# A planned kernel: what the plan charges for TensorE's products and for its changes of tiling

## The chip, the cores and the metric

The kernel runs on one core of one Trainium2 chip. The metric is device time in microseconds (us) of one execution; each time shown is one run, and medians are over runs.

## What is computed

A trunk of two layers over 256 context tokens and 512 latent tokens, 1024 channels, all in fp32. Each layer modulates and normalises its input, projects it once, and feeds three mixers side by side:

```python
conv_l, q_l, k_l, v_l, rw_l, gate_l = _split(hl @ lp['w_in'], IN_SPLITS)
y_att_l = _att_post(_diff_attend(q_lat, keys_l, vals_l, lam), lp['att_subln_g'], lambda_init)
y_conv_l = _conv_branch(conv_l, *conv_args)
y_rw_c, y_rw_l = _rwkv_branch(rw_c, rw_l, lp, need_ctx)
out_l = _merge(y_conv_l, y_att_l, y_rw_l, gate_l, lp)
xl = xl + gl1 * ol
xl = xl + gl2 * _sqrelu_mlp(_modulate(xl, norm2_g[l], shl2, scl2), mlp_w1[l], mlp_w2[l])
```

The three mixers are a depthwise convolution of 31 taps, differential attention with 4 heads, and RWKV-7, a recurrence run in both directions. A gated merge, an output projection and a squared-ReLU MLP follow. The second layer drops the context tokens after they have been read. A last normalisation gives the output, latent tokens alone.

## The kernel before

Activations lie with channels on the 128 partitions and tokens along the free axis. A weight matrix is cut into units of 128 output channels. A unit's product over the 512 latent tokens (and, where the context counts, over its 256) runs as three reduced-precision products: each fp32 operand is split into a high and a low part (wh and wl, hh and hl), and hh*wh, hl*wh, hh*wl are summed in PSUM under the name mmps. The weights come in as wr by DMA, ScalarE copies them to wh, VectorE subtracts to get wl. These big products fill the whole 128x128 array.

RWKV's recurrence is computed in chunks of 64 tokens, by small fp32 products that use a part of the array (64 or 32 rows or columns): lps and aps (low-rank inputs), tps (the matrices of a chunk), tvps, wps and jps (solving them), ca, cb and psy (the chain that carries the state X from chunk to chunk). An fp32 product shows as two records in the trace, a reduced one and a transpose as one. There are 16 halves (8 in each layer), with 6 chunks each. A step of the chain goes ca<-x,ar on TensorE, an addition into rhs on VectorE, ca<-rhs,j and cb<-rhs,j on TensorE, copies into gv, ca<-gv,tok on TensorE, and an addition that makes the next x. The outputs psy of a step are computed in the next step's first wait (y_products).

**How the order is made.** The whole order of all engines is fixed when the program is built. Each part of the work is a generator, a stream, with a letter. `weave` keeps a planned clock for each engine. Again and again it asks every stream when its next piece could start, and lets the earliest one issue; within EPS = 0.02 us the one that stands first in a string of letters wins (ORDER_A = "CIEKAWLRGT" in the RWKV stage of layer 0: C is the chain, K and R prepare chunks, W converts weights, G issues the big products, T the convolution's taps on VectorE). A stream names the time its data is due, the engine, and maybe a lead: the chain gives STICK = 0.2 us ahead of the groups behind rhs and gv, so that it is taken up to 0.2 us before its data is due.

```python
t = max(s[1], self.clock[s[2]] + s[5], held) - s[5]
if best is None or t < at - EPS:
    best, at, got, since = s, t, names, held
```

The stream that is taken issues its instructions and calls `spend`, which moves the engine's planned clock by the piece's charge and returns the end plus SEM = 0.19 us, the time at which others may use the result. The charges are formulas: `Timed.cost` for VectorE, ScalarE and GpSimd (elements / 960, 1200 and the like, plus a constant), `load` for DMAs, `product` and `turn` (a transpose) for TensorE. Only the order that comes out matters: real waits are semaphores.

Before, `product` (L227) charges columns / 2400 us + 0.003 for a reduced product and for an fp32 one four passes, scaled by output width for small ones. A full-width product gets 0.06 us more when the one before it was charged less than 0.1 us (`self.short`). The second of two products that run side by side on different rows (`beside`) is charged 0.004. `turn` (L239) charges 0.119.

The stages in time: a head (0 to 107 us), the RWKV stage woven with the input projection of layer 0 (107 to 595), attention, convolution and the remaining projection units (to about 905), merge, output projection and MLP (to about 1600), the norm and the start of layer 1 (to 1705), its RWKV stage (to 2215), its attention (to 2390), its merge and MLP, and the last norm.

Of the kernel before, what the change touches and what calls it, by code (L numbers as in the profile page):

```python
# [19 lines left out]
P = 128  # L20
# [31 lines left out]
SPARE = 1.5  # L52
EPS = 0.02
STICK = 0.2
BLK = 1040
CTX = (0, NCTX)
LAT = (NCTX, NLAT)
# [63 lines left out]
class Trunk:  # L121
# [15 lines left out]
    def setup(self):  # L137
# [29 lines left out]
        nc.vector.tensor_tensor(out=self.cc, in0=self.cc, in1=sg, op=ALU.mult)  # L167
        self.blk_in = [self.dram.tile([96 * BLK], F32, name=f"bin{i}") for i in range(2)]
        self.blk_out = [self.dram.tile([96 * BLK], F32, name=f"bout{i}") for i in range(2)]
        self.blk = 0  # L170
# [56 lines left out]
    def product(self, out, lhsT, rhs, at=None, beside=0, **kw):  # L227
        self.nc.tensor.matmul(out, lhsT, rhs, **kw)  # L228
        m, n = lhsT.free_size(), rhs.free_size()
        c = n if rhs.dtype == F32R else 4 * n * max(m, 32) / P  # L230
        cost = (max(0.027, c / 2400) + 0.003) if not beside else 0.004
        if rhs.dtype != F32R:
            cost = max(cost, 0.1 if m == P else 0.0) + (0.012 if 32 < n <= P else 0.04 if n > P else 0.0)
        if self.short and m == P:
            cost += 0.06
        self.short = cost < 0.1
        return self.spend("PE", cost, at)

    def turn(self, out, src):  # L239
        self.nc.tensor.transpose(out, src, self.ident)  # L240
        return self.spend("PE", 0.119)

    def load(self, out, in_, q=None, rate=360e3):

# [167 lines left out]
    def start(self):  # L412
        self.queues, self.closing, self.n_queued = [], False, 0
        self.plan, self.after, self.after_over, self.n_after = [], deque(), False, 0
        self.n_load = self.n_conv = self.n_used = 0
        self.banks = dict(lat=deque([0.0, 0.0]), ctx=deque([0.0]))
        self.ring = dict(lat=deque([self.mm, self.mm]), ctx=deque([self.mm]))
        self.gone = dict(lat=deque(), ctx=deque())
        self.raws, self.parts = deque([self.wp] * WR), deque([self.wp] * WC)
        self.locks, self.t0, self.now, self.todo, self.short = {}, 0.0, 0.0, [], False  # L420
        self.shared, self.shared_t = 0, 0.0

    def enqueue(self, i, q):
# [643 lines left out]
    def half_t(self, n, pp, hh, prep, c0):  # L1067
# [38 lines left out]
        def blocks(x):  # L1106
            return x.rearrange("(p x) -> p x", x=BLK)[:, 0:1024].rearrange("p (i w) -> p i w", w=64)[:, :, 0:16]

        def rows(x, g):
            return x[g * 48 * BLK:(g + 1) * 48 * BLK].rearrange("(n y) -> n y", y=4 * BLK)[:, 0:4096].rearrange(  # L1110
                "n (s t) -> s n t", t=64)
# [197 lines left out]
    def chain_piece(self, pi, st, y, need_y):  # L1309
# [5 lines left out]
        for q in range(2):  # L1315
# [11 lines left out]
            else:  # L1327
# [10 lines left out]
                t = V.tensor_tensor(out=rhs, in0=ga[:, 0:128], in1=tv[:, q, :], op=ALU.add)  # L1338
                yield t, "PE", None, None, STICK
            gps = [ga[:, 256:384], gb[:, 0:128]]  # L1340
# [8 lines left out]
            yield from self.y_outs()  # L1349
            yield t, "PE", None, None, STICK  # L1350
            if not last:
# [206 lines left out]
    def phase_a(self, l, full, lat, esh, esf, eps):  # L1558
        nc = self.nc
        c0 = self.c0 = lat[0][0]  # L1560
        with ExitStack() as es:
# [19 lines left out]
            if l == 0:  # L1581
                z = self.pa.tile([P, T], F32, tag="stage", name="zero", bufs=1)[0:96, 0:BLK // 2]
                nc.gpsimd.memset(z, 0.0)
                for t in self.blk_out:
                    for h in range(2):
                        nc.gpsimd.dma_start(out=t.rearrange("(p h x) -> p h x", h=2, x=BLK // 2)[:, h], in_=z)
            self.weave(ORDER_A[l], dict(C=self.chain(l, c0), I=self.inverse(), R=self.prepare(l, c0),
# [732 lines left out]
```

## Time and profile before

| | |
|---|---|
| median of 3 runs | 2911.05 us (2907.64 to 2918.86) |
| the profiled execution | 2907.25 us, its span 2905.5 us |
| instructions | 56275 |
| TensorE busy | 2770.2 us, 95% |
| VectorE busy | 1951.0 us, 67% |
| ScalarE busy | 1298.6 us, 45% |
| GpSimd busy | 105.5 us, 4% |

The span runs from the first to the last instruction of the profiled execution. Matmuls overlap: a big product with 512 columns is recorded for some 0.39 us, while the next one starts 0.23 us later, so what a product costs is read from start to start. "Idle before" is time in which no recorded instruction of the engine ran. PEclk is the granted share of TensorE's full clock of 2.4 GHz.

### The profile page before, as it was taken

Reading aid. Unit: us, or ns where it says so; the run is one execution under the profiler, and the core shown is the slowest. Engines: PE = TensorE matmul, PEld = TensorE weight load, DVE = VectorE, ACT = ScalarE, POOL = GpSimd, SP = SyncE. Lnnn points to the kernel's source line nnn. Section 1 sums busy time; section 2 is a strip of 40 time slices with the busy share of each in tenths; the row PEclk is TensorE's granted clock in tenths of the full one; section 3 lists DMA queues with packets and bytes.
Section 4 is the critical chain, followed back from the end, with each engine's and each line's share of the span. In section 5 each row is a group of like instructions: output and inputs, shape, how many; then the busy total and the mean of one; then the engine's idle time right before and its main releaser. Section 6 shows DMA issues by size and latency. Waiting matters only on the chain.

```text
span 2905.5 us, 56275 instructions
## 1 busy us (share of the span) xinstructions
PE 2770.2 (95%) x22423; PEld 2234.9 (77%) x22423; DVE 1951.0 (67%) x4230; ACT 1298.6 (45%) x2522; POOL 105.5 (4%) x181
## 2 busy tenths in 40 slices
PE   8999999998999999999999999999999889899998
PEld 6777777776788887888888777777777667788887
DVE  6778777489995558764333569889985766644445
ACT  4556655555544224231313346555554663433333
POOL 0000000010000000000000000001000100000000
PEclk9999999999999999999999999999999999999999
DMA  5232223354237733553112313233235436322223
GB/s 211 66 77 70 72 81 90 102 158 120 83 111 267 255 124 111 181 187 110 63 65 68 101 60 91 64 87 83 77 108 177 140 103 203 134 96 95 95 96 104
DMA packets 248903, 333.05 MB, mean 115 GB/s; under 512 B 118385, under 2 KB 124161, under 8 KB 248513
## 3 DMA queue, kind: packets, MB, share of 16 engines
q1 hardware_dynamic: 243312, 313.73, 34.2%
q0 software_dynamic: 3712, 14.17, 1.9%
q8 instruction: 176, 2.88, 0.4%
q10 hardware_dynamic: 1616, 1.56, 0.2%
q14 instruction: 87, 0.70, 0.1%
HBM read 267.37 MB, written 48.65 MB: 109 GB/s over the span
## 4 chain that ended last, share of the span: by engine, by line
PE 72%; DVE 13%; ACT 5%; DMA 3%; issue 2%; SPq 1%; POOL 0%; DVEq 0%; ACTq 0%; POOLq 0%
PE mmps L228 59%; PE ca L228 3%; DVE cacc L92 2%; DVE wl L92 2%; ACT wh L92 1%; PE tps L228 1%; PE sps L228 1%; PE psy L228 1%; PE wps L228 1%; PE jps L228 1%; DVE x L92 1%; DVE ast L92 1%; DMA j<-bout 1%; DMA akm<-akl 1%; PE tvps L228 1%
## 5 line engine op out<-in xcount | busy, mean ns | idle before, releaser
L228 PE MATMUL mmps<-hh,wh 128*128 128x512 f32 (+1 forms) x2344 | 850.0, 363 | 23.9 <-ACT wh L92 5.8
L228 PE MATMUL mmps<-hh,wl 128*128 128x512 f32 (+1 forms) x2344 | 844.8, 360 | 9.0 <-DVE wl L92 8.8
L228 PE MATMUL mmps<-hl,wh 128*128 128x512 f32 (+1 forms) x2344 | 844.3, 360 | 4.1 <-DVE hl L92 3.8
L92 DVE TENSOR_TENSOR wl<-wr,wh 128x512 fp32r<-128x512 f32 x596 | 411.5, 691 | 480.6 <-ACT wh L92 469.0
L92 ACT ACTIVATE wh<-wr 128x512 fp32r<-128x512 f32 x596 | 375.2, 630 | 714.9 <-PE mmps L228 664.9
L228 PEld LDWEIGHTS mmps<-hh,wh 128*128 128x128 f32 x2344 | 447.9, 191 | 95.0 <-issue 18.0
L228 PEld LDWEIGHTS mmps<-hh,wl 128*128 128x128 f32 x2344 | 446.9, 191 | 80.9 <-DVE wl L92 16.2
L228 PEld LDWEIGHTS mmps<-hl,wh 128*128 128x128 f32 x2344 | 447.6, 191 | 67.9 <-DVE hl L92 7.2
L228 PE MATMUL mmps<-ffl,wh 128*128 128x512 f32 (+1 forms) x792 | 279.2, 353 | 0.0
L228 PE MATMUL mmps<-ffh,wh 128*128 128x512 f32 (+1 forms) x792 | 278.1, 351 | 0.0
L228 PE MATMUL mmps<-ffh,wl 128*128 128x512 f32 (+1 forms) x792 | 277.0, 350 | 0.0
L92 DVE SCALAR_TENSOR_TENSOR cacc<-upad,dww,cacc 128x783 f32<-128x783 f32 (+1 forms) x240 | 215.2, 897 | 4.5
L228 PEld LDWEIGHTS mmps<-ffh,wh 128*128 128x128 f32 x792 | 149.1, 188 | 22.7
L228 PEld LDWEIGHTS mmps<-ffh,wl 128*128 128x128 f32 x792 | 148.9, 188 | 21.5
L228 PEld LDWEIGHTS mmps<-ffl,wh 128*128 128x128 f32 x792 | 149.4, 189 | 20.7
L92 DVE SCALAR_TENSOR_TENSOR x<-mmps,mod,x 128x512 f32<-128x512 f32 (+1 forms) x126 | 80.0, 636 | 45.5 <-PE mmps L228 45.0
L92 POOL TENSOR_TENSOR bk<-bk,pc 128x384 f32<-128x384 f32 x64 | 58.0, 937 | 1198.9 <-PE tps L228 1140.0
L92 DVE SCALAR_TENSOR_TENSOR sq<-mmps,rl 128x512 f32<-128x512 f32 x96 | 56.9, 596 | 40.4 <-ACT rl L92 40.4
L92 ACT ACTIVATE stage<-mmps 128x512 f32<-128x512 f32 (+1 forms) x116 | 59.0, 510 | 50.8 <-PE mmps L228 45.9
L92 ACT ACT_TABLE_LOAD x62 | 79.5, 1283 | 4.7 <-PE mmps L228 2.6
L92 DVE TENSOR_REDUCE ast<-sps 128x1 f32<-128x768 f32 (+1 forms) x80 | 65.6, 845 | 21.6 <-PE sps L228 21.5
L92 ACT ACTIVATE rl<-mmps 128x512 f32<-128x512 f32 x96 | 49.3, 515 | 67.9 <-PE mmps L228 67.9
(329 smaller groups left out, 4371.1 us busy)
## 6 DMA issues: line engine op xcount, KB each, us to landing
wr<-in_w_dram SPq DMA_DIRECT2D x268, 256.0 KB, 2.5
wr<-in_win_dram SPq DMA_DIRECT2D x236, 256.0 KB, 2.8
modw<-in_modw_dram SPq DMA_DIRECT2D x80, 512.0 KB, 4.5
wr<-in_pw_dram SPq DMA_DIRECT2D x48, 256.0 KB, 2.9
wr<-in_wo_dram SPq DMA_DIRECT2D x44, 256.0 KB, 2.6
g<-stage SPq DMA_DIRECT2D x24, 384.0 KB, 3.2
gate<-g SPq DMA_DIRECT2D x24, 384.0 KB, 4.0
scb<-in_modw_dram SPq DMA_DIRECT2D x16, 512.0 KB, 6.3
```

Of the source, the lines that this page charges most:

```text
L92: f(**kw)
L228: self.nc.tensor.matmul(out, lhsT, rhs, **kw)
```

## The change

The charges of TensorE in the plan are replaced. A product is `part` when it uses fewer than 128 columns or rows of the array. A change from whole to part is charged ENTER = 0.09 us, from part to whole LEAVE = 0.2 us, in place of the 0.06 us. A column is charged 1/2246 us rather than 1/2400, a transpose 0.108 us. The least charge of an fp32 product is 0.22 us if it uses the whole array, 0.1 us if it is full in width and part in rows (0.1 us for both before), and none beside the general least of 0.024 + 0.003 us (0.027 + 0.003 before) if it is narrow. No instruction, tile or buffer is added or taken away; the order that the weaver makes can differ on every engine.

```diff
@@ -52,6 +52,9 @@
 SPARE = 1.5
 EPS = 0.02
 STICK = 0.2
+
+ENTER = 0.09
+LEAVE = 0.2
 BLK = 1040
 CTX = (0, NCTX)
 LAT = (NCTX, NLAT)
@@ -227,18 +230,21 @@
     def product(self, out, lhsT, rhs, at=None, beside=0, **kw):
         self.nc.tensor.matmul(out, lhsT, rhs, **kw)
         m, n = lhsT.free_size(), rhs.free_size()
+        part = m < P or lhsT.shape[0] < P
         c = n if rhs.dtype == F32R else 4 * n * max(m, 32) / P
-        cost = (max(0.027, c / 2400) + 0.003) if not beside else 0.004
+        cost = max(0.024, c / 2246) + 0.003 if not beside else 0.004
         if rhs.dtype != F32R:
-            cost = max(cost, 0.1 if m == P else 0.0) + (0.012 if 32 < n <= P else 0.04 if n > P else 0.0)
-        if self.short and m == P:
-            cost += 0.06
-        self.short = cost < 0.1
+            cost = max(cost, 0.0 if m < P else 0.1 if part else 0.22) + (0.012 if 32 < n <= P else 0.04 if n > P else 0.0)
+        if part != self.part:
+            cost += ENTER if part else LEAVE
+            self.part = part
         return self.spend("PE", cost, at)
 
     def turn(self, out, src):
         self.nc.tensor.transpose(out, src, self.ident)
-        return self.spend("PE", 0.119)
+        cost = 0.108 + (LEAVE if self.part else 0.0)
+        self.part = False
+        return self.spend("PE", cost)
 
     def load(self, out, in_, q=None, rate=360e3):
 
@@ -417,7 +423,7 @@
         self.ring = dict(lat=deque([self.mm, self.mm]), ctx=deque([self.mm]))
         self.gone = dict(lat=deque(), ctx=deque())
         self.raws, self.parts = deque([self.wp] * WR), deque([self.wp] * WC)
-        self.locks, self.t0, self.now, self.todo, self.short = {}, 0.0, 0.0, [], False
+        self.locks, self.t0, self.now, self.todo, self.part = {}, 0.0, 0.0, [], False
         self.shared, self.shared_t = 0, 0.0
 
     def enqueue(self, i, q):
```

## Rows read from the trace of the kernel before

**Rows 1.** The page: the span, and its part 1 (busy time by engine).
```profile
span 2905.5 us, 56275 instructions
...
PE 2770.2 (95%) x22423; PEld 2234.9 (77%) x22423; DVE 1951.0 (67%) x4230; ACT 1298.6 (45%) x2522; POOL 105.5 (4%) x181
```

**Rows 2.** Windows by stage: stretch, length, busy us (x records) by engine, PEclk, DMA.
```profile
107.00:595.00 488.00, 469.21 (x6345) 368.95 (x6343) 349.92 (x1022) 270.77 (x591) 34.83 (x57) 0.99 0.32 85
1705.00:2215.00 510.00, 494.29 (x6091) 370.29 (x6091) 438.11 (x1166) 275.72 (x595) 33.79 (x48) 1.00 0.31 85
2215.00:2390.00 175.00, 150.51 (x641) 112.41 (x641) 122.43 (x199) 109.13 (x199) 18.57 (x36) 0.92 0.52 153
1200.00:1600.00 400.00, 400.00 (x2285) 350.54 (x2284) 180.78 (x292) 102.20 (x169) 0.64 (x2) 1.00 0.31 106
```

**Rows 3.** Timeline of TensorE at 2700 us: start, us, instruction.
```profile
2700.16 0.40 PE L228 MATMUL mmps<-ffl,wh 128*128 128x512 f32 x1
2700.39 0.39 PE L228 MATMUL mmps<-ffh,wl 128*128 128x512 f32 x1
```

**Rows 4.** Timeline of TensorE, 433 to 437 us: one step of the chain.
```profile
433.66 0.44 PE L228 MATMUL ca<-x,ar 128*64 128x128 f32 x4
434.03 0.38 PE L228 MATMUL mmps<-hh,wl 128*128 128x256 f32 x1
434.25 0.28 PE L228 MATMUL mmps<-hh,wh 128*128 128x256 f32 x1
...
434.72 0.28 PE L228 MATMUL mmps<-hl,wh 128*128 128x256 f32 x1
434.93 0.27 PE L228 MATMUL ca<-rhs,j 64*64 64x64 f32 x1
...
435.31 0.38 PE L228 MATMUL mmps<-hh,wl 128*128 128x256 f32 x1
435.53 0.28 PE L228 MATMUL mmps<-hh,wh 128*128 128x256 f32 x1
...
435.86 0.45 PE L228 MATMUL ca<-gv,tok 128*64 128x64 f32 x8
```

**Rows 5.** Timeline of VectorE, 430 to 436.5 us.
```profile
430.85 0.56 DVE L92 TENSOR_TENSOR bk<-t,e 128x384 f32<-128x384 f32 x1
431.33 0.55 DVE L92 TENSOR_TENSOR bk<-a,e 128x384 f32<-128x384 f32 x1
...
434.31 0.28 DVE L92 TENSOR_TENSOR rhs<-ca,tv 128x128 f32<-128x128 f32 x1
```

**Rows 6.** Groups of TensorE's instructions: count | busy, mean ns | idle before, releasers.
```profile
L228 PE MATMUL ca<-gv,tok 128*64 128x64 f32 x704 | 40.5, 235 | 1.7 <-ACT gv L92 1.6
...
L228 PE MATMUL ca<-rhs,j 64*64 64x64 f32 x352 | 38.8, 230 | 5.0 <-DVE rhs L92 4.0
L228 PE MATMUL ca<-x,ar 128*64 128x128 f32 x352 | 38.6, 297 | 1.2 <-DVE x L92 0.9
```

**Rows 7.** Timeline of TensorE: first and last entry into small tiles, 365 in all.
```profile
107.91 1.16 PE L228 MATMUL tps<-ar,bk 64*128 64x128 f32 x16
...
2212.44 0.34 PE L228 MATMUL psy<-tr,gv 128*64 128x64 f32 x4
```

**Rows 8.** Waits of TensorE: what waited, for what: us, times, longest us.
```profile
PE mmps L228 <- DVE wl L92: 9.9, 12, 3.2
...
PE sps L228 <- DMA akl<-akl: 6.6, 5, 2.9
PE sps L228 <- ACT ap L92: 5.9, 7, 1.8
PE mmps L228 <- ACT wh L92: 5.8, 5, 3.3
...
PE atps L240 <- ACT aat L92: 4.2, 6, 1.3
PE atps L240 <- DVE ap L92: 4.2, 3, 2.9
```

## The prediction

> **What bounds the kernel now.** I read the page first: TensorE is busy 2770.2 of 2905.5 us, so it idles 135.3 us and no other engine is near it [rows 1]. The reader is to see there that only three things can move the time: TensorE's idle time, time at the low clock, and time lost at changes of tiling. Its products themselves stay the same, as the change edits charges in the plan and not one instruction.
>
> Next the windows by stage [rows 2]. "Phase A" is the stretch in which RWKV's small products are woven between the big ones of the input projection: 107 to 595 us in layer 0 and 1705 to 2215 us in layer 1. TensorE is busy 469.21 of 488 and 494.29 of 510 us there, so it waits 34.5 us in both, at a granted clock of 0.99 and 1.00 (2.4 GHz nearly all the time). Attention of layer 1 (2215 to 2390 us) waits 24.5 of 175 us, and its granted clock is 0.92. In the MLP (1200 to 1600 us) it never waits.
>
> Then the timeline, for pitches. Two big products with 512 columns start 0.23 us apart [rows 3], with 256 columns 0.12 us (434.25 onward) [rows 4]. Entering the small tiles costs extra: the last big product before them starts at 434.72, the first small one at 434.93, 0.21 us against 0.12, so 0.09. Leaving costs 0.22 against 0.12 behind the first big product (435.31 to 435.53), and about 0.10 more ahead of it: 0.2. These are the numbers that the new constants hold.
>
> **What the plan believed, and will believe.** One step of the chain, from 433.66 to 435.86 [rows 4], took 2.20 us. An fp32 product shows as two records, so the four records of ca<-x are two products. Old charges: 2 x 0.122 for ca<-x, 6 x 0.110 for the six big products, 4 x 0.068 for the rhs group, 0.06 + 3 x 0.110 for the last three: 1.56 us, 71% of the real time. New charges: 2 x 0.129, 0.2 + 6 x 0.117, 0.09 + 4 x 0.072, 0.2 + 3 x 0.117: 2.09 us, 95%. Summed in this way over all products of both phase A stretches [rows 2], the old charges come to 414 and 431 us, the new ones to 471 and 496, against busy times of 469 and 494. VectorE was already charged its pitch: two 128x384 operations start 0.48 us apart [rows 5], charged 0.47. So the old plan ran TensorE some 15% too fast against the other engines; the new one runs them alike.
>
> TensorE: Matmul & The Clock Gate of the Trainium skill, section "Wait — 56ns, not 53.3ns?", gives N / 2.4 GHz + 2.5 ns, which is 0.216 us at 512 columns: the old charge, and it speaks against the new one. This trace does not agree, its pitch is 0.23 [rows 3]. By the page, the 448 big products that stay in the waits of part 1 below would each be charged 0.015 us too much, an estimate of 7 us more of stalls, and the sum would end at 2912 us; by the row nothing is added.
>
> **Part by part.** The weaver takes the stream that can start first; the cost of a change of tiling is charged only after a choice, so it steers nothing directly. What changes is how many big products fit into a wait of the chain.
>
> 1. Fewer big products per wait. For the groups behind rhs and gv the weaver stops filling STICK, 0.2 us, before the data is due. In the example rhs ends at 434.59 [rows 5] and its group starts at 434.93, a slack of 0.34 us. I went through all groups ca<-x, ca<-rhs and ca<-gv [rows 6] (88, 88 and 88 places) in time; 165 have big products ahead of them. Stopping the fill where the right clock would stop it takes out 132 of 580 big products there (24 us of filling), and the idle time ahead of those groups goes from 5.6 to 8.3 us: **+2.7 us**. The 24 us aren't saved: those products run later, in attention or behind it. Bounds: 0, and 0.2 us for each of the 176 groups with STICK, 35 us. I take 2.7, since it rests on these very places.
>
> 2. Changes of tiling. Phase A enters the small tiles 172 + 193 = 365 times, counted from the first to the last [rows 7], at 0.09 + 0.2 us each. A group that comes ready while TensorE is in small tiles is joined to them. With leaving charged, the plan spends 42% of phase A in or around small tiles rather than 38%; of some 192 groups that don't hang on the chain (per half: lps, aps, three tps, three tvps, four solves; 16 halves) 4% more, eight, join: 8 x 0.29 = **-2.3 us**. Bounds: 0 and 192 x 0.29 = -56; near 0, since nothing in the choice looks for it.
>
> 3. Big products that wait for converted weights. TensorE waits 9.9 us for wl and 5.8 for wh [rows 8]. With the engines' plans in step, fewer conversions stand behind a VectorE or ScalarE operation that is still waiting for a product. Bounds 0 and -15.7; I take a quarter, **-3.9 us**, nearer to 0: only phase A, a third of the span, has charges that change by more than 7%.
>
> 4. Attention. Products here are charged 5% more (130 to 136 us for layer 1), so the cover over each wait shrinks. 21 waits (akl 5, ACT ap 7, aat 6, DVE ap 3) come to 20.9 us [rows 8]. If each was covered for about 3 us, 5% are 0.15 us: 21 x 0.15 = 3.2. Bounds 0 and 3.2; half, **+1.5 us**.
>
> 5. MLP, merge, head: every product scaled alike, so their order and the gaps stay. Nothing, hidden by TensorE's own queue; if that cover were gone, VectorE at 180.78 of 400 us [rows 2] has room.
>
> Sum: +2.7 - 2.3 - 3.9 + 1.5 = -2.0 us. The profiled execution took 2907.25 us around its span of 2905.5, 0.13% under the median of 2911.05. 2907.25 - 2.0 = **2905 us**. A measurement of this kernel can tell about 0.5%, 14.5 us, from no change.
>
> **Rivals.**
>
> *Faster: long waits vanish.* The six waits of [rows 8] hold 36.6 us, and attention of layer 1 loses 175 x 0.08 = 14 us to the low clock of 1.2 GHz that follows them [rows 2]. They come of an order that doesn't fit the real times; a plan in step could undo half of both: 18 + 7 = 25 us, 2882 us. For it: the sums of the new charges meet the busy times within 1%. Against it: these waits lie mostly outside phase A, where the charges change by 5 to 7% alone. Perfetto Trace Analysis of the Trainium skill, "Identifying the Most-Contended Engine", wants TensorE's headroom judged by the weight loads' busy share, not the matmuls'. By it there is more room: weight loads are busy 76% and 73% in phase A against 88% in the MLP, 135 us in all by [rows 2].
>
> *Slower: the old error was a cushion.* As TensorE really ran 15% behind its plan, data was mostly there when it came. With the cushion gone, each of the 176 groups behind rhs and gv can stall for up to STICK. At half of that, 0.1 us, 176 x 0.1 = 18 us and 2925 us; it decides from 14.5 / 176 = 0.08 us each. For it: in the example the new charges put 0.29 us of entering and leaving into a wait whose slack is 0.34. Against it: 48 of the 88 rhs groups have no big product ahead of them at all, small ones fill their wait, and the waits today come to 5.0 and 1.7 us [rows 6].
>
> *It does not do what it says.* The order is largely set by what depends on what. Then the orders differ little and the time is that of before, 2907; this lies within the forecast's case.
>
> **How the numbers follow.** Forecast, no change that can be told: 0.42, its own range 2890 to 2920. Faster rival 0.33, as every charge moves toward the trace. Slower rival 0.25. Range: on the fast side two thirds of the waits and the clock (33 us) give 2874; on the slow side 0.14 us a stall gives 2932; about 0.1 is left beyond either end. Faster by over 0.5% 0.33, within 0.42, slower 0.25.
>
> **What would show it.** Right: phase A is shorter by some 10 us in each layer while fills move behind it; rhs groups wait more than 5.0 us, to about 8; entries into small tiles fall from 365 by about eight; total idle within 10 us of 135. Faster rival: wl, akl and ap waits fall by half and attention's clock rises over 0.92. Slower rival: idle ahead of ca<-rhs and ca<-gv above 20 us. The forecast is wrong if total idle or the number of entries moves by more than a tenth.

## The result: slower by 2.65%, and the profile after

Over six runs the changed kernel takes 2986.81 us (2975.58 to 2996.01) against 2910.30 us of before: a ratio of 1.0265, 95% interval 1.0246 to 1.0283. The forecast was 2905 us with a range up to 2932. Its profiled execution took 2990.15 us, 82.9 us more than the one of before.

The page of the changed kernel, its span and part 1:

```profile
span 2988.4 us, 56305 instructions
...
PE 2806.5 (94%) x22423; PEld 2258.3 (76%) x22423; DVE 1953.1 (65%) x4230; ACT 1296.8 (43%) x2522; POOL 105.0 (4%) x181
```

Against [rows 1]: the same 22423 matmul records, and yet TensorE is busy 36.3 us longer, and idle 46.6 us longer. The other engines do the same work in the same busy time. So all of it is time lost between the same products.

For a comparison stage by stage, both RWKV stages are cut at the same marks now: from the first lps to the last psy. Windows of before, layer 0 and layer 1:

```profile
86.20:562.60 476.40, 460.53 (x6320) 361.83 (x6320) 351.19 (x1040) 264.65 (x587) 30.14 (x48) 1.00 0.29 77
1711.00:2213.00 502.00, 486.29 (x6063) 364.02 (x6062) 433.95 (x1158) 273.36 (x590) 33.79 (x48) 1.00 0.31 84
```

The same windows of the changed kernel:

```profile
84.70:551.20 466.50, 434.89 (x6071) 336.14 (x6071) 345.48 (x1030) 253.34 (x566) 31.37 (x48) 0.97 0.27 69
1765.80:2236.20 470.40, 433.81 (x5765) 321.95 (x5765) 398.37 (x1106) 253.07 (x555) 31.82 (x48) 0.98 0.28 73
```

The stages became shorter, by 9.9 and 31.6 us, which looks like a gain. But 249 and 298 records are missing from them: big products, which now run later. The groups by line show it, one third of the filling each, in layer 0 and then layer 1 of before:

```profile
L228 PE MATMUL mmps<-hh,wh 128*128 128x256 f32 (+1 forms) x443 | 157.0, 354 | 3.6 <-DVE r L92 1.6 <-DVE k L92 0.9 <-DVE stage L92 0.8
L228 PE MATMUL mmps<-hh,wh 128*128 128x512 f32 (+1 forms) x437 | 166.3, 381 | 0.1
```

and of the changed kernel:

```profile
L231 PE MATMUL mmps<-hh,wh 128*128 128x256 f32 (+1 forms) x360 | 129.2, 359 | 3.4 <-DVE k L95 1.6 <-DVE stage L95 0.6 <-DVE r L95 0.5
L231 PE MATMUL mmps<-hh,wh 128*128 128x512 f32 (+1 forms) x339 | 129.1, 381 | 0.0
```

At the pitches of [rows 3, 4], 0.231 us for 512 columns (the median of the MLP) and 0.12 for 256, the filling in both stages is worth 495.9 us before (1614 and 1026 products) and 386.5 after (1218 and 876). That gives the measure used from here on: **the length of both stages less their filling**, that is small products, changes of tiling, waits and clock. It is 978.4 - 495.9 = 482.5 us before and 936.9 - 386.5 = 550.4 after: 68 of the 83 us are lost here. Idle time gives 36.6 of them (from 15.87 + 15.71 to 31.61 + 36.59). The granted clock, 0.97 and 0.98 where it was 1.00, gives about 20: 41 us of these stages run at 1.2 GHz, half of the full clock. Entries into small tiles fell from 174 + 193 to 161 + 179, 27 x 0.29 = 8 us gained, an estimate at the price of [rows 4]. The remaining 19 us are left by subtraction: time between the starts of products that is neither idle nor clock, see the last section.

A good part of the waits is ahead of the chain's groups. The same lines as [rows 6], after:

```profile
L231 PE MATMUL ca<-gv,tok 128*64 128x64 f32 x704 | 44.2, 241 | 5.1 <-ACT gv L95 2.9 <-DVE gv L95 1.5
...
L231 PE MATMUL ca<-x,ar 128*64 128x128 f32 x352 | 40.2, 303 | 9.2 <-DVE x L95 8.0
L231 PE MATMUL ca<-rhs,j 64*64 64x64 f32 x352 | 39.3, 232 | 13.7 <-DVE rhs L95 12.3 <-DVE upad L769 0.5
```

28.0 us ahead of these three groups where it was 7.9: 20.1 of the 36.6 us. VectorE is named for most of it. It isn't slower at its work, it comes late to it: the rhs operation starts a median of 0.54 us after the start of its product's last record, 0.40 before (88 places each; the quickest place has 0.31 in both). But coming late is not enough for a loss: in a kernel below that loses nothing (the change x 0.87) the median is 0.56, and the wait is short all the same.

```profile
L231 PE MATMUL ca<-rhs,j 64*64 64x64 f32 x352 | 38.9, 231 | 6.5 <-DVE rhs L95 5.2
```

What that kernel has more of is filling: 2752 big products in both stages, 2094 in the changed kernel. The timeline of VectorE in the changed kernel, at the step of [rows 4], has an example of a late operation:

```profile
435.21 0.27 DVE L95 TENSOR_SCALAR gv<-cb 64x128 f32<-64x128 f32 x1
436.18 0.75 DVE L95 SCALAR_TENSOR_TENSOR v<-mmps,pvl,v 128x511 f32<-128x511 f32 x1 [0.70 <-ACT v L95]
436.85 0.28 DVE L95 TENSOR_TENSOR x<-ca,xp 64x128 f32<-64x128 f32 x1
```

The product of x (ca<-gv,tok) ended at 436.04. The operation for x stands in VectorE's queue behind one on v that waits 0.70 us for ScalarE, so x starts 0.81 us after its product; in the kernel before, at the same step, 0.12 us after. The order is fixed: one late operation can hold up whatever was planned behind it.

The other 15 us lie mostly in the merge of layer 0, 219.3 us where it took 207.2: its modulation products wait 5.5 us for weights, and the clock falls to 0.98. The stretch from layer 0's RWKV stage to its merge loses about 8 us more, net of filling, and layer 1's merge gains about 7. The merge of layer 0 before and after:

```profile
896.50:1103.70 207.20, 201.56 (x1569) 170.99 (x1568) 114.40 (x205) 63.95 (x104) 0.00 (x0) 1.00 0.60 209
936.00:1155.30 219.30, 208.65 (x1565) 172.02 (x1564) 98.97 (x186) 50.32 (x88) 0.00 (x0) 0.98 0.57 197
```

### The profile page after: what moved, and what is told of

Same layout as the page of the kernel before. It is cut to its first block, busy times and chain, and to the rows that moved or that the text cites. A ratio compares the mean times of both kernels' runs of the same rounds, so it can differ in the third digit from the quotient of the medians.

```text
span 2988.4 us, 56305 instructions
## 1 busy us (share of the span) xinstructions
PE 2806.5 (94%) x22423; PEld 2258.3 (76%) x22423; DVE 1953.1 (65%) x4230; ACT 1296.8 (43%) x2522; POOL 105.0 (4%) x181
## 5 line engine op out<-in xcount | busy, mean ns | idle before, releaser
L231 PE MATMUL mmps<-hh,wh 128*128 128x512 f32 (+1 forms) x2344 | 850.9, 363 | 20.4 <-DVE k L95 6.4
L95 DVE TENSOR_REDUCE ast<-sps 128x1 f32<-128x768 f32 (+1 forms) x80 | 65.4, 845 | 20.4 <-PE sps L231 20.2
L95 DVE TENSOR_TENSOR ffl<-sq,ffh 128x768 fp32r<-128x768 f32 (+1 forms) x64 | 52.8, 825 | 38.8 <-ACT ffh L95 38.6
```

The lines of the kernel that those rows point to most:

```text
L95: f(**kw)
```

## The experiments

Theory 1: all charges of TensorE together set how fast its planned clock runs against the other engines' clocks; slower means less filling in each wait, and the cushion goes. Theory 2: charging the changes of tiling in lumps does it. All times are medians, with the ratio to the kernel before from the same chip. "Loss" is the measure above, less the 482.5 us of before; "fill" counts big products in both stages (2640 before).

| kernel | us | ratio, 95% interval | fill | loss, us |
|---|---|---|---|---|
| the change | 2986.8 | 1.0265, 1.0246 to 1.0283 | 2094 | 68 |
| column pitch alone | 2937.0 | 1.0103, 1.0078 to 1.0128 | 2419 | 28 |
| tiling charges alone | 2947.9 | 1.0138, 1.0115 to 1.0161 | 2410 | 43 |
| the change x 0.87 | 2909.8 | 1.0003, 0.9990 to 1.0017 | 2752 | 6 |
| before x 1.15 | 3007.3 | 1.0342, 1.0315 to 1.0368 | 2308 | 65 |
| the change, SEM 0.30 | 2957.9 | 1.0168, 1.0142 to 1.0193 | 2442 | 41 |
| the change, STICK 0 | 2994.2 | 1.0295, 1.0266 to 1.0325 | 2191 | 63 |
| the change x 0.80 | 2957.1 | 1.0169, 1.0144 to 1.0194 | 2909 | -9 |
| before x 0.90 | 2969.8 | 1.0216, 1.0181 to 1.0251 | 3064 | -5 |
| x 0.87 in the RWKV stages alone | 2927.9 | 1.0072, 1.0054 to 1.0091 | 2752 | 9 |
| the chain taken 0.2 us late | 2991.5 | 1.0295, 1.0263 to 1.0328 | 2204 | 59 |
| VectorE x 1.15 | 2936.2 | 1.0096, 1.0078 to 1.0113 | 2684 | 17 |
| VectorE, ScalarE, GpSimd x 1.15 | 2939.3 | 1.0107, 1.0091 to 1.0124 | 2531 | 26 |
| the change x 0.93 | 2931.3 | 1.0067, 1.0052 to 1.0082 | 2448 | 33 |
| x 0.80 in layer 0's RWKV stage, x 0.87 elsewhere | 2914.6 | 1.0016, 1.0004 to 1.0029 | 2767 | -1 |
| VectorE x 1.15 and SEM 0.30 | 2936.8 | 1.0091, 1.0071 to 1.0111 | 2813 | 9 |

**The two halves of the change.** The column pitch alone, on the kernel before:

```diff
-        cost = (max(0.027, c / 2400) + 0.003) if not beside else 0.004
+        cost = (max(0.027, c / 2246) + 0.003) if not beside else 0.004
```

> The column pitch alone (1/2246 us a column in place of 1/2400), changes of tiling charged as before. Charges of big products rise by 6.5%, of the whole of phase A by about 5%. Theory 1 (the speed of TensorE's planned clock against the other engines sets how much filling lies in each wait, and every slowing of it takes cushion away): a third of the loss, 2930 to 2945 us. Theory 2 (charging changes of tiling in lumps does it): 2905 to 2915 us.

and the changes of tiling alone (ENTER and LEAVE as in the change, in `turn` too):

```diff
-        if self.short and m == P:
-            cost += 0.06
-        self.short = cost < 0.1
+        part = m < P or lhsT.shape[0] < P
+        if part != self.part:
+            cost += ENTER if part else LEAVE
+            self.part = part
```

> ENTER and LEAVE alone, all products at the charges of before. Phase A's charges rise by about 9%. Theory 1 (planned speed of TensorE): two thirds of the loss, 2950 to 2970 us. Theory 2 (the lumps): all of it, 2980 to 2990 us.

2937.0 and 2947.9 us, the second 2 us under the range of theory 1. Each does harm by itself, the one that adds more to the charges the more, and together nearly the whole: 1.03% and 1.38% of 2.65%. The pitch has nothing to do with lumps, so theory 2 fails as the only cause.

**The same proportions at the old speed, and the old proportions at the new speed.** In the changed kernel, and with 1.15 in the kernel before (`turn` alike):

```diff
-        return self.spend("PE", cost, at)
+        return self.spend("PE", 0.87 * cost, at)
```

> The changed kernel with every charge of TensorE times 0.87, ENTER and LEAVE among them: the same proportions, the planned speed of before. Theory 1: 2900 to 2920 us, some 1300 filling products in phase A of layer 0. Theory 2: still 2960 us or more. A third theory (the old charges had proportions that happened to suit the chain): 2940 or more as well.

> The kernel before with every charge of TensorE times 1.15: the old proportions, the planned speed of the changed kernel. Theory 1: 2970 to 3000 us, with fewer than 1150 filling products in phase A of layer 0. Theory 2: 2905 to 2920 us.

These two decide it. Scaled by 0.87, the change costs nothing (1.0003); the old charges scaled by 1.15 lose even more than the change does, a little over what was expected, with 1166 fillings in layer 0 where under 1150 were forecast. Of the 97 us that its profiled execution took more than the one of before, 65 lie in the RWKV stages and 31 between layer 0's RWKV stage and its merge, net of filling. The windows of the scaled change, layer 0 and 1:

```profile
84.40:580.90 496.50, 476.15 (x6379) 374.79 (x6379) 357.60 (x1043) 275.83 (x599) 31.51 (x48) 0.99 0.28 76
1709.60:2220.30 510.70, 495.55 (x6115) 374.09 (x6115) 435.71 (x1163) 277.19 (x597) 33.54 (x48) 1.00 0.32 86
```

and of the kernel before with 1.15:

```profile
86.10:556.30 470.20, 438.12 (x6159) 339.32 (x6158) 348.67 (x1034) 259.79 (x576) 30.22 (x48) 0.99 0.27 70
1765.10:2270.40 505.30, 463.06 (x5893) 343.04 (x5892) 424.81 (x1146) 261.17 (x569) 32.92 (x48) 0.97 0.27 72
```

Length less busy time: 20.4 and 15.2 us in the first, near the 15.9 and 15.7 of before; 32.1 and 42.2 in the second, as in the changed kernel. What the proportions are hardly matters here; how fast the whole planned clock of TensorE runs does.

**Which slack is missing.** Longer hand-overs, and no early commitment, both on the changed kernel:

```diff
-SEM = 0.19
+SEM = 0.3
```

> The changed kernel with SEM, the planned delay from one engine's end to the next engine's start, at 0.30 us in place of 0.19; TensorE's charges stay those of the change. If the loss is that planned waits are too short for the real ones, with TensorE's speed only the old remedy: waits are planned 0.22 us longer per hand-over pair, filling comes back and the time falls to 2900 to 2930 us. If exact charges do harm in another way, it stays above 2960 us.

```diff
-STICK = 0.2
+STICK = 0.0
```

> The changed kernel with STICK = 0, so that the groups behind rhs and gv are taken when their data is due by the plan, no longer up to 0.2 us ahead. If the early commitment to these 176 groups is the loss, 2910 to 2930 us. If every wait of phase A is too tight, the x groups and the solves among them, it falls by a third at most: 2955 to 2975 us.

Longer hand-overs bring back over a third, 2957.9 us, between the two outcomes stated. STICK at 0 brings nothing back, 2994.2 us: less than either theory gave it. So the lead that the forecast blamed in its slower rival isn't the fault by itself. A margin ahead of the chain's own groups is no remedy either:

```diff
-STICK = 0.2
+STICK = -0.2
...
-            yield self.x_t, "PE"
+            yield self.x_t, "PE", None, None, STICK
```

> The changed kernel with the chain's three groups (x, rhs, gv) taken 0.2 us after the planned time of their data, in place of 0.2 us ahead (rhs, gv) and at it (x); all charges those of the change. If it is slack ahead of the chain's own groups that is missing: filling comes back by one or two products at each of 264 places, 2910 to 2935 us. If the delay sits in the other groups too (solves, tps, tvps, weights), 2945 us or more.

2991.5 us, so the delay sits in other groups too, by the expectation. The waits for x are hardly shorter than in the changed kernel (8.0 us there), those for rhs are (12.3 there):

```profile
PE ca L231 <- DVE rhs L95: 7.6, 20, 1.6
PE ca L231 <- DVE x L95: 7.3, 20, 0.7
```

The loss of 59 us stays even so: shorter waits ahead of rhs alone don't win the time back. Charging VectorE more does (in the second kernel the factor holds for ScalarE and GpSimd too):

```diff
-            return self.trunk.spend(self.name, self.cost(op, kw), at)
+            return self.trunk.spend(self.name, self.cost(op, kw) * (1.15 if self.name == "DVE" else 1.0), at)
```

> The changed kernel with VectorE's charges times 1.15, all others those of the change. If VectorE runs behind its plan and the chain's groups wait for its queue, the plan makes room for that: 2920 to 2945 us, stalls ahead of ca<-rhs and ca<-x at 10 us or less. If VectorE's charges are right and any wait is just too tight by chance, less than a third comes back: 2960 us or more.

> VectorE's, ScalarE's and GpSimd's charges times 1.15, TensorE's those of the change: nearly the ratio of before, with SEM and the DMA charges left alone. If the ratio of TensorE to the other engines is all that counts: 2905 to 2925 us. If the hand-over and DMA times must be stretched as well: 2930 to 2955 us.

2936.2 us, two thirds of the loss back, and 51 of the 68 us in the RWKV stages. The waits in the kernel with VectorE x 1.15:

```profile
PE ca L231 <- DVE rhs L95: 7.8, 21, 0.8
PE ca L231 <- DVE x L95: 2.2, 9, 0.3
```

Those for x fall from 8.0 to 2.2 us, those for rhs from 12.3 to 7.8, no further than with the margin; the groups wait 9.2 and 2.9 us in all, a little over the 10 that was expected. Stretching ScalarE and GpSimd as well adds nothing: 2939.3 us, not the 2905 to 2925 that were expected if the ratio of TensorE to the other engines were all that counts, but the 2930 to 2955 for hand-overs and DMA times that would have to be stretched too. No run stretches all of these together. Longer hand-overs and VectorE x 1.15 together:

```diff
-SEM = 0.19
+SEM = 0.3
...
-            return self.trunk.spend(self.name, self.cost(op, kw), at)
+            return self.trunk.spend(self.name, self.cost(op, kw) * (1.15 if self.name == "DVE" else 1.0), at)
```

> The changed kernel with VectorE's charges times 1.15 and SEM at 0.30 together. Alone they gave 2936 and 2958 us. If VectorE's work and the hand-overs are two separate parts of what the plan leaves out, their returns add up: 2905 to 2920 us. If both only stand for one cushion that is full by then, 2925 to 2945 us.

They don't add up in time, 2936.8 us. In the RWKV stages the loss falls to 9 us, less than the sum of what each returned (51 and 27 of 68), as one cushion that is full by then would have it. What is left lies outside of these stages: layer 1's attention waits 34.4 us in this kernel, and 24.5 in the kernel before [rows 2], and the merge of layer 0 is as slow as in the changed kernel.

**Where it is lost.** The factor 0.87 while the RWKV stages are planned, 1 elsewhere:

```diff
-        return self.spend("PE", cost, at)
+        return self.spend("PE", self.rate * cost, at)
...
+            self.rate = 0.87
             self.weave(ORDER_A[l], dict(C=self.chain(l, c0), I=self.inverse(), R=self.prepare(l, c0),
...
+            self.rate = 1.0
```

> The changed kernel with TensorE's charges times 0.87 while the two RWKV stages (phase A) are planned, and at the new charges everywhere else. If the whole loss is made in phase A: 2900 to 2920 us, as with the factor everywhere. If attention, merge and head have a share: 2925 to 2950 us.

2927.9 us: 59 of the 77 us come back. Of the 18 that are left, 9 lie in the RWKV stages themselves and some 8 in layer 1's attention, net of filling; the differences of the other stages are under 5 us each and nearly cancel. So most of the loss is made while the RWKV stages are planned, though the time is not that of the factor everywhere.

**How it grows, and the other side.** The same edit with 0.93 and 0.80 on the change, and with 0.90 on the kernel before:

> The changed kernel with every charge of TensorE times 0.93, half way between 0.87 (2910 us) and 1.00 (2987 us). If the loss grows with each product that is taken out of a wait: 2935 to 2960 us. If it sets in at a point, 2910 to 2920 or 2970 and more.

> The changed kernel with every charge of TensorE times 0.80, a planned speed 7% above that of before. If more cushion still pays, 2885 to 2900 us; if the cushion of before already covers the waits, 2900 to 2915 us with some more filling in phase A and idle time there under 15 us a layer.

> The kernel before with every charge of TensorE times 0.90. As for the factor 0.80 on the changed kernel: 2885 to 2900 us if more cushion still pays, 2900 to 2915 us if it is used up; above 2920 us if filling for too long delays the chain so far that the projection's products run out in it.

0.93 gives 2931.3 us, a little under what steady growth would have, with 33 us lost in the stages (ahead of ca<-rhs it waits 15.1 us, even more than the changed kernel); 6, 33 and 68 us at 0.87, 0.93 and 1: the loss in the stages grows steadily from about the speed of before on. Still faster planned clocks miss what was hoped of them: 2957.1 and 2969.8 us, though the RWKV stages lose 9 and 5 us less than before. Most of the price is paid in layer 1's attention. Its window in the kernel with 0.80, and then its share of filling (a third):

```profile
2269.20:2426.30 157.10, 114.73 (x442) 80.74 (x438) 106.95 (x174) 89.38 (x162) 18.55 (x36) 0.82 0.47 136
```

```profile
L231 PE MATMUL mmps<-hh,wh 128*128 128x512 f32 x50 | 21.1, 423 | 1.5 <-ACT wh L95 1.5
```

42.4 us of waits and a granted clock of 0.82, where before waited 24.5 us at 0.92 with 104 such products: the RWKV stage used up the filling, and half as much is left for the waits of attention. The second price is layer 0's merge, from its first product to the first of the MLP, before and with 0.80 (309.7 us in the kernel before x 0.90):

```profile
896.50:1180.70 284.20, 273.04 (x1962) 232.08 (x1961) 182.56 (x334) 96.03 (x159) 0.00 (x0) 0.99 0.55 187
898.40:1199.10 300.70, 287.26 (x1967) 243.52 (x1966) 201.04 (x352) 99.76 (x164) 0.00 (x0) 0.93 0.53 176
```

To tell this from harm in the RWKV stage itself, 0.80 was kept for layer 0 alone, which has filling to spare:

```diff
+            self.rate = 0.87 if l else 0.8
             self.weave(ORDER_A[l], dict(C=self.chain(l, c0), I=self.inverse(), R=self.prepare(l, c0),
...
+            self.rate = 0.87
```

> The changed kernel with TensorE's charges times 0.80 in the RWKV stage of layer 0 and times 0.87 everywhere else. If the loss of the factor 0.80 everywhere (2957 us) is made in layer 1, where the filling runs out before attention does: 2900 to 2920 us, attention of layer 1 waiting 20 to 28 us in place of 42. If over-filling harms the RWKV stage itself, 2930 us or more. It is also the candidate for a kernel faster than both.

2914.6 us, as expected, and its attention of layer 1 waits 28.7 us, a little over the 20 to 28 named:

```profile
2216.70:2379.60 162.90, 134.23 (x587) 98.74 (x583) 114.32 (x187) 102.96 (x187) 18.55 (x36) 0.95 0.54 161
```

So the factor 0.80 in layer 0's RWKV stage costs next to nothing by itself. This run doesn't split the rest, as it holds 0.87 in layer 1's stage and outside both: the merge of layer 0 takes 283.1 us in it. No kernel of the study is faster than the one before; two come within 0.2%.

## Why the prediction was wrong

Its view of what bounds the kernel held, and so did its sums: the new charges are near the real pitch. The step that failed is part 1 of the sum, which priced the filling that goes at 2.7 us and looked for its price at the chain's groups alone; with it went the sign of the whole. Its own sign of being wrong came: total idle moved from 135.3 to 181.9 us. A shorter phase A, which it named as a sign of being right, came too (9.9 and 31.6 us), with a slower kernel.

- **Part 1, fewer big products per wait: +2.7 us said, 68 us found for the RWKV stages net of all gains.** It went through the places in the trace of before as they stood and took filling away only ahead of the chain's groups, 132 products. 546 went. The chain's groups wait 28.0 us in place of 7.9, 20.1 more; the forecast had 8.3 for 165 of these places. Its upper bound, 35 us, would have covered the chain's groups. It was too low for the whole, because what it left out pays as well: the solves (wps waits 10.1 us for jt, 5.4 before), tps and the clock.
- **Part 2, changes of tiling:** right in sign, 27 entries fewer rather than eight, some 8 us at the forecast's price of 0.29 each.
- **Part 3, waits for weights: no gain.** wl 10.9 and wh 5.2 us, against 9.9 and 5.8 [rows 8].

```profile
PE mmps L231 <- DVE wl L95: 10.9, 13, 2.8
PE wps L231 <- DVE jt L95: 10.1, 10, 1.5
...
PE sps L231 <- ACT ap L95: 7.9, 8, 2.0
...
PE sps L231 <- DMA akl<-akl: 6.2, 5, 3.9
...
PE mmps L231 <- ACT wh L95: 5.2, 7, 2.0
```

- **Part 4, attention:** waits shifted between operations (ap 7.9, akl 6.2). Layer 1's has no loss net of filling; layer 0's stretch up to the merge waits 29.4 us, 19.7 before, more than the +1.5 said for both. **Part 5:** the MLP is as before; "nothing" was wrong for the merge of layer 0, 12 us.
- **The rivals.** The slower one named the mechanism, a cushion that goes, and was given 0.25. It put the place in STICK's lead, which the run with STICK 0 doesn't bear out, and its price, 18 us, was too small by three quarters. Its sign, over 20 us of idle time ahead of ca<-rhs and ca<-gv, was nearly met: 18.8, from 6.7. The faster rival leaned on the charges meeting the trace; with the factor 0.87 they miss it, and the loss is gone.
- **The page of the Trainium skill cited against the change** (TensorE: Matmul & The Clock Gate, "Wait — 56ns, not 53.3ns?") would have put the sum at 2912 us. Its direction was right by luck: its pitch, 0.216 us at 512 columns, isn't the 0.231 of this trace.

Shown: TensorE's planned speed makes the loss (0.87 and 1.15), mostly in the RWKV stages, and stretching VectorE's plan returns most of what is lost there. Not shown: why VectorE needs room there. Its charges agree with its pitch in the pair of [rows 5]. Stops behind waiting operations, as the one at 436.18, are there; but the 88 rhs operations start 29.0 us later in all than at the quickest place's delay, and in 25.6 of these VectorE works on other operations. In the kernel with 0.87 it is 26.2 and 24.5 us. No run takes the stops or this crowding away, so the cause stays open.

## What to carry to other kernels

Where a planner fixes the order of engines that run without a common clock, the charge of the engine that should never wait can also be the cushion of the plan, as it was here: made exact, with no allowance elsewhere, it lost 2.65%. Don't trust a charge because it meets the trace. Scale the bottleneck's charges and measure both sides: here too slow a plan stalled it among the small products, and too fast a plan spent the filling that a later stage needed. A stage that becomes shorter hasn't gained until the work that left it is counted.

## What was not expected of the hardware

TensorE was busy 36.3 us longer on the same 22423 records. Part of it, about 20 us, is time at the low clock in the RWKV stages. For the rest, a record can hide a wait: a 512-column product is recorded for 0.39 us while the next can start after 0.23 [rows 3], so a wait of up to 0.16 us behind it would leave no idle time in the profile. Not all of the rest is behind big products: at the full clock, and with idle time left out, the records of small products in these stages start 30.3 ns apart in the mean, 28.9 before, over some 9000 of them. Stalls of a fine weave have to be read from start to start.

The granted clock was 1.00 in both RWKV stages of before and fell six times in those of the changed kernel, to 1.2 GHz for 41 us in all. Each fall came behind a stretch with solves (wps, jps) and waits of TensorE; ahead of the first, at 167.8 us, it had waited 2.22 us for j. More idle time in a stage did not mean a lower clock: with SEM 0.30 the stage of layer 1 is idle 7.4% of its length at a mean of 1.00, where layer 0's in the changed kernel is idle 6.8% at 0.97.

```profile
1737.50:2241.10 503.60, 466.19 (x5945) 345.80 (x5944) 426.34 (x1150) 265.99 (x575) 31.44 (x48) 1.00 0.29 77
```
